# w_out's second parts, the expert choice and expert 0's preparation placed otherwise in an encoder kernel on one core

## The chip, the core and the metric

The kernel runs on one core of a Trainium2 chip. The core has TensorE (PE, matrix products, with a queue of its own for weight loads), VectorE (DVE), ScalarE (ACT), GpSimd (POOL) and SyncE (SP, whose queue issues most of the transfers); each works through its own instructions in order and waits on semaphores for the others. The metric is the time of one execution on the device in microseconds (us), taken as the median of several.

## The reference, cut to what matters

One layer of an encoder runs over two request groups, 512 and 1024 tokens of 1024 channels, with shared weights, all in float32:

```python
h   = rmsnorm(x, norm1_g)
z   = h @ w_in                                # conv value, conv gate, pooling input
yc  = silu(layernorm(depthwise_conv31(za * sigmoid(zg)) + conv_b))
yp  = (centred_mean(zp, windows 2, 4, 8, 16) - zp) @ pool_w * pool_scale
x   = x + concat(yc, yp) @ w_out
h   = rmsnorm(x, norm2_g)
p   = softmax(h @ w_router)                   # 16 experts
gates, idx = top_k(p.T, 2 * tokens // 16)     # each expert picks 64 or 128 tokens of a group
ye  = (silu(h[idx] @ w_gate) * (h[idx] @ w_up)) @ w_down * gates
x   = x.at[idx].add(ye)
x   = x + sigmoid(x @ w_pg + b_pg) * (p_in @ w_ple)
y   = rmsnorm(x, final_g)
```

## The kernel before, in words

A float32 product is made of three passes: each operand is split into a first part (the value rounded to the form that PE multiplies at full rate) and a second part (the value less the first), and first x first, second x first and first x second are added in PSUM. A split takes a copy on ScalarE (first part) and a subtraction on another engine (second part).

The program is emitted in one order, and each engine runs its own instructions in that order.

- **The projection loop** (24 steps). Each step multiplies tokens by a slice of w_in (L103 to L105) and feeds the convolution. A part of the 31 taps runs on PE (L413), on shifted copies of u: `u_shift` loads u from DRAM four times, shifted by one each (L404, on SP's queue). The other taps run on DVE (L427 to L434). Layer norm over channels is made by `ln_steps`, whose inverse square root is a Newton iteration of small operations on GpSimd (L153 to L156, L527, L528). GpSimd also makes the running sums of the pooling heads (L447) and stores (L488, L547). Within steps 18, 20 and 22, `wo_split` (L574) splits eight rows of w_out, 128x1024 each, three, three and two to a step. The rows arrive in buffers of the pool `stg` (name `st`), loaded by `wo_load` (L572) and, for parts of the conv output, by `y_load` (L557). These loads are on SP's queue too, so a load that waits for a buffer holds what stands behind it.
- **Segments 0 to 47**: the product with w_out (`w_mm`, L606 to L608), twelve products a segment, four segments to each of twelve token blocks. Functions are entered in a table `AT` by segment (`at(segment, function, ...)`) and run in the order in which they were entered, behind the segment's products: the residual add (`x1_half`, L613, DVE), transposes of the sum (`x1_T`, L642, PE), the router (`route`, L661; `route_sum`, L669), its softmax (`softmax`, L671 to L680) and the transposition of the probabilities (`probs_T`, L690 or L693, PE).
- **Expert choice.** `topk_steps` finds the top entries of a list by rounds of three DVE instructions (L702 maximum of eight, L703 their places, L704 strike them out): 16 rounds on the list "s" (tokens of the longer group, 512 wide), 8 on the list "p" (256 wide). At the end of every segment `topk` adds a budget to a credit and emits rounds until the credit is used up; a round is booked at 3 x (0.14 + width / 960) us, which is 2.02 and 1.22. When a list is done, its transposition (`merge_T`, L717 on PE and L719 on DVE), its merge (`merge`, L725, L730 to L734) and the gather of expert 0's tokens (`gather`, L746, GpSimd) are entered for later segments, counted from the one in which it ended.
- **Segments 48 to 71**: the product of the second input with w_ple (`ple_mm`, L990 to L992), six products (two half-blocks of three) a segment, with `ple_T` (L976) for the transposes, `ple_out` (L1001, ACT, for half of the last blocks DVE, L999) for the copies out, and the preparation of expert 0: loads of its weights (`load`, L920), their split (`split_hi` on ACT, L937; `split_lo` on DVE, L946), and the transposes of its tokens (`turn0`, L776 and L778, in four parts, copied out at L781 and L782).
- **Experts**: 16 experts with L1187 (gate and up projection) and L1224 to L1240 (down projection); then the last product, with w_pg, and the final norm.

`weights()` opens three pools in the room that earlier pools leave: the raw expert weights (`raw`) and two for the split ones. A tile that is placed where an older tile lay waits for the older one's last reader.

The names in what follows: `wb` and `st`, split and raw w_out rows; `u`, the conv input; `nm`, the softmax's negative scaled maximum; `fs` and `fp`, the lists' results; `prb` and `pr`, probabilities; `xTe`, expert 0's transposed tokens (and, in the ple part, the second input).

## Time and profile before

| | |
|---|---|
| time of an execution, median of 3 | 2300.36 us (2298.39 to 2300.44) |
| the profiled execution's own time | 2296.16 us |
| its span, first to last instruction | 2294.4 us |
| granted TensorE clock, mean of the span | 0.995 |
| PE busy | 2238.4 us (98%) |
| PE weight loads busy | 1906.6 us (83%) |
| DVE busy | 1734.6 us (76%) |
| ACT busy | 1403.3 us (61%) |
| POOL busy | 271.1 us (12%) |

The profile comes from one execution. Busy time is the time in which an engine has an instruction under way. The places of the stages on the time axis: the projection loop runs to about 303 us, segments 0 to 47 from 303.7 to 478.7, segments 48 to 71 from 478.7 to 527.3, the experts from 528.9 to about 2105. A granted clock of 1.00 means TensorE's full 2.4 GHz, 0.50 the half of it.

### The profile page before, as it was taken

The page shows a single profiled execution, that of the slowest core. Times are in us where ns is not written, and L with a number is a line of the kernel's source. Part 1 is how long each engine was busy: PE and PEld are TensorE (multiplying, and loading weights), DVE is VectorE, ACT ScalarE, POOL GpSimd, SP SyncE. Part 2 cuts the span into 40 slices and gives each one's busy share as a digit, 9 for nine tenths or more (in the row PEclk, how much of TensorE's full clock was granted, in tenths as well). Part 3 has the DMA queues.
Part 4 walks back from the last instruction along what each step waited for, and adds up shares of the span by engine and source line. Part 5 has one row for each costly group of instructions (what it writes and reads, how often), then busy time and mean ns, then how long its engine had stood idle before and what let it go on. Part 6 is the DMA issues. An engine that isn't in the chain of part 4 may idle for free.

```text
span 2294.4 us, 36978 instructions
## 1 busy us (share of the span) xinstructions
PE 2238.4 (98%) x15062; PEld 1906.6 (83%) x15106; DVE 1734.6 (76%) x2326; ACT 1403.3 (61%) x1835; POOL 271.1 (12%) x534
## 2 busy tenths in 40 slices
PE   7999999989999999999999999999999999999997
PEld 6888867768798988889898888979888897988675
DVE  8798863667787878778787877878787777878565
ACT  4324336447666766766676676666666767666443
POOL 0122232221001010100101010010101001000321
PEclk9999999999999999999999999999999999999999
DMA  6434555557777677777767777777777777667442
GB/s 199 109 115 123 170 160 188 184 217 265 282 259 277 260 266 280 244 280 265 269 268 260 281 248 274 272 262 267 262 280 255 268 278 256 272 243 275 142 138 101
DMA packets 168874, 534.26 MB, mean 233 GB/s; under 512 B 11969, under 2 KB 38625, under 8 KB 168704
## 3 DMA queue, kind: packets, MB, share of 16 engines
q1 hardware_dynamic: 156064, 493.70, 58.7%
q0 software_dynamic: 9040, 31.46, 5.6%
q10 hardware_dynamic: 3600, 6.74, 0.8%
q8 instruction: 118, 1.93, 0.3%
q14 instruction: 52, 0.43, 0.1%
HBM read 481.34 MB, written 50.52 MB: 232 GB/s over the span
## 4 chain that ended last, share of the span: by engine, by line
PE 77%; issue 10%; DVE 5%; DMA 4%; ACT 2%; POOL 1%; SPq 0%; DVEq 0%; ACTq 0%; POOLq 0%
PE pg L1187 27%; PE pg L1191 13%; PE S L1224 9%; PE Pp L1224 4%; PE S L1234 4%; PE Pp L1240 2%; PE pz L103 2%; PE pz L105 2%; PE pz L104 2%; PE pz L413 2%; PE po L1377 1%; PE po L1376 1%; PE po L1379 1%; DMA u<-u_d 1%; PE pz L606 1%
## 5 line engine op out<-in xcount | busy, mean ns | idle before, releaser
L946 DVE TENSOR_TENSOR wl<-raw,wh 128x2048 bf16<-128x2048 f32 x388 | 881.8, 2283 | 62.8 <-issue 54.9
L1187 PE MATMUL pg<-xTe,wh 128*128 128x384 f32 x4096 | 775.7, 340 | 2.6 <-ACT wp L1001 1.6
L937 ACT ACTIVATE wh<-raw 128x2048 fp32r<-128x2048 f32 x388 | 736.0, 1909 | 39.2 <-DMA raw<-in_w_up_dram 21.9
L1187 PEld LDWEIGHTS pg<-xTe,wh 128*128 128x128 f32 x4096 | 699.9, 188 | 9.4 <-ACT ye_s L1289 6.2
L1191 PE MATMUL pg<-xTb,wl 128*128 128x192 bf16 x4096 | 382.8, 247 | 0.0
L1191 PEld LDWEIGHTS <-wl 128*128 128x128 bf16 x4096 | 325.2, 98 | 40.3 <-issue 40.3
L1250 ACT ACTIVATE t<-pg 128x384 f32<-128x384 f32 x256 | 125.8, 491 | 298.9 <-PE pg L1191 284.1
L1224 PE MATMUL S<-wh,hT 128*128 128x512 f32 x1024 | 285.5, 398 | 0.6 <-ACT ye_s L1289 0.6
L1251 DVE TENSOR_TENSOR t<-pg,t 128x384 f32<-128x384 f32 x256 | 142.7, 557 | 157.7 <-ACT t L1250 157.4
L1224 PEld LDWEIGHTS S<-wh,hT 128*128 128x128 f32 x1024 | 186.4, 188 | 36.8 <-ACT ye_s L1289 1.0
L103 PE MATMUL pz<-xTh,wb 128*128 128x256 f32 x576 | 165.4, 287 | 0.6 <-ACT xTh L212 0.4
L104 PE MATMUL pz<-xTl,wb 128*128 128x256 f32 x576 | 163.0, 283 | 1.5 <-DVE xTl L213 1.5
L105 PE MATMUL pz<-xTh,wb 128*128 128x256 f32 x576 | 163.0, 283 | 0.7 <-DVE wb L241 0.7
L1224 PE MATMUL Pp<-wh,hT 128*128 128x512 f32 x512 | 161.0, 390 | 0.8 <-DVE ye_p L1293 0.8
L746 POOL DMA_INDIRECT xg_s<-h_s,idx_s x16 | 24.2, 1514 | 1160.8 <-PE pg L778 579.1
L429 DVE SCALAR_TENSOR_TENSOR acc<-u,kT,acc 128x496 f32<-128x496 f32 (+2 forms) x168 | 126.9, 755 | 5.1
L103 PEld LDWEIGHTS pz<-xTh,wb 128*128 128x128 f32 x576 | 110.3, 192 | 10.9 <-issue 5.8
L1224 PEld LDWEIGHTS Pp<-wh,hT 128*128 128x128 f32 x512 | 96.1, 188 | 22.4 <-DVE ye_p L1293 1.2
L782 DVE SCALAR_TENSOR_TENSOR xTe<-pg,vT,xTe 128x128 fp32r<-128x128 f32 (+1 forms) x120 | 49.5, 412 | 86.0 <-ACT xTe L781 83.9
L104 PEld LDWEIGHTS pz<-xTl,wb 128*128 128x128 f32 x576 | 110.4, 192 | 1.9 <-DVE xTl L213 1.7
L105 PEld LDWEIGHTS pz<-xTh,wb 128*128 128x128 f32 x576 | 110.4, 192 | 0.9 <-DVE wb L241 0.9
L1234 PE MATMUL S<-wl,hTb 128*128 128x512 bf16 x480 | 108.8, 379 | 2.2
(293 smaller groups left out, 2652.7 us busy)
## 6 DMA issues: line engine op xcount, KB each, us to landing
raw<-in_w_gate_dram SPq DMA_DIRECT2D x128, 1024.0 KB, 6.5
raw<-in_w_up_dram SPq DMA_DIRECT2D x128, 1024.0 KB, 7.9
raw<-in_w_down_dram SPq DMA_DIRECT2D x128, 1024.0 KB, 6.2
u<-u_d SPq DMA_DIRECT2D x32, 262.0 KB, 5.8
st<-yT_d SPq DMA_DIRECT2D x12, 512.0 KB, 5.6
pl<-ple_d SPq DMA_DIRECT2D x12, 512.0 KB, 4.6
out_dram<-raw SPq DMA_DIRECT2D x11, 512.0 KB, 2.9
st<-in_w_out_dram SPq DMA_DIRECT2D x8, 512.0 KB, 4.9
```

The source lines that it names most:

```text
L103: nc.tensor.matmul(out, wh, xh, start=first, stop=False)
L104: nc.tensor.matmul(out, wh, xl, start=False, stop=False)
L105: nc.tensor.matmul(out, wl, xh, start=False, stop=last)
L429: nc.vector.scalar_tensor_tensor(acc[:, :n], u[:, s:s + n], kT[:, c, s:s + 1], acc[:, :n], op0=OP.mult, op1=OP.add)
L937: nc.scalar.activation(h, src, AF.Copy)
L946: nc.vector.tensor_sub(l, src, h.bitcast(F32))
L1187: nc.tensor.matmul(pg[:, f, 0:384].rearrange("p (a t) -> p a t", a=2), h[:, k, f * P:(f + 1) * P], xT[:, k, :, c], start=(k == 0), stop=False)
L1191: nc.tensor.matmul(pg[:, f, 0:192], l[:, k, f * P:(f + 1) * P], xb[:, k, c], start=False, stop=(k == KD - 1))
L1224: nc.tensor.matmul(out[:, n, :], x, rhs(h, i, n), start=(k == 0 and first), stop=(out is Pp and k == KF - 1))
L1234: nc.tensor.matmul(S[:, n, :], hT[1][:, k, so:so + CS], rhs(l, i, n), start=False, stop=(k == KF - 1))
L1250: nc.scalar.activation(t, pg[:, :, 192:384], AF.Copy)
L1251: nc.vector.tensor_add(t, pg[:, :, 0:192], t)
```

## The change

Seven edits in one file:

1. `wo_split`: the subtraction of the eight w_out rows is issued to GpSimd instead of DVE.
2. `softmax`: the product `nm * r` of two 128x1 tiles is written as tensor_scalar, with `r` as the scalar operand, instead of tensor_mul.
3. `topk`: the budget of a segment is 2.9 us instead of 2.35 up to segment 47, and 2.5 instead of 1.25 from 48 on. The 16 rounds of list "s" then end in segment 45 instead of 47, the 8 of list "p" in 55 instead of 58; the entries that are counted from there move with them (`merge_T` "s" from segment 52 to 49, its merge and gather from 54 to 51; `merge_T` "p" from 60 to 56, its merge and gather from 61 to 57).
4. `probs_T` of blocks 8, 9 and 10 is entered one segment later, `h2_out` of block 11 one segment earlier.
5. `turn0`: parts 0 to 3 in segments 66, 67, 68, 69 instead of 68, 69, 68, 70. The loads of the first expert weights: segments 50, 51, 52, 54, 57, 60, 64 instead of 52, 58, 55, 52, 62, 64, 68. `weights()` in segment 48 instead of 50, with the pool `raw` opened first, so that it lies lowest.
6. A new function `sig_table` in segment 56: a sigmoid of one column, whose result nobody reads.
7. The PSUM pools psD and psG of the expert phase are opened in the other order.

```diff
--- before.py
+++ after.py
@@ -577,7 +577,7 @@
         h, l = WO[k // 3][0][:, k % 3, :], WO[k // 3][1][:, k % 3, :]
         r = WOR.pop(k)
         nc.scalar.activation(h, r, AF.Copy)
-        nc.vector.tensor_sub(l, r, h.bitcast(F32))
+        nc.gpsimd.tensor_sub(l, r, h.bitcast(F32))
 
     LATER = (4, 5, 6, 7, 10, 11)
     X, O, HT, LG, PR, RR = {}, {}, {}, {}, {}, {}
@@ -672,7 +672,7 @@
         pl, r = LG.pop(i), RR[i]
         nm = small.tile([P, 1], F32, name="nm")
         nc.vector.tensor_reduce(nm, pl, axis=AX.X, op=OP.max, negate=True)
-        nc.vector.tensor_mul(nm, nm, r)
+        nc.vector.tensor_scalar(nm, nm, r, None, op0=OP.mult)
         pr = prb[:, i % 2, 32:48] if i in LATER else small.tile([P, NE], F32, name="pr")
         sm = small.tile([P, 1], F32, name="sum")
         nc.scalar.activation(pr, pl, AF.Exp, bias=nm, scale=r, accum_out=sm)
@@ -1063,10 +1063,15 @@
     def weights():
         nonlocal hlp, hlp2, rawp
         lft.close()
+        rawp = lpool("raw", 2)
         hlp = lpool("hl", 4)
         hlp2 = lpool("hl2", 6)
-        rawp = lpool("raw", 2)
         WPL["o2"] = lpool("po", 1, lpo).tile([P, 2, D], F32, name="wo2")
+
+    def sig_table():
+
+        t = small.tile([P, 1], F32, name="nm")
+        nc.scalar.activation(t, g1T[:, 0:1], AF.Sigmoid)
 
     OB = 14
     for i in range(12):
@@ -1087,10 +1092,10 @@
         at(max(a + 5, t + 2), route, i)
         at(max(a + 5, t + 2) + 1, route_sum, i)
         at(max(a + 6, t + 3), softmax, i)
-        at(max(a + 7, t + 1), h2_out, i)
+        at(max(a + 7 - i // 11, t + 1), h2_out, i)
         if i < 8:
             at(max(a + 12, t + 1), w_load, i + 4)
-        at(t + 5 if i not in (7, 11) else a + 7 + i // 11, probs_T, i)
+        at(t + 5 if i < 7 else a + 8 if i > 7 else a + 7, probs_T, i)
         if i == 7:
             at(a + 7, list_add, "s")
         elif i == 11:
@@ -1099,10 +1104,11 @@
                     (6, conv1, (2, 3)), (8, conv2, (2, 3)), (8, conv_out, (2, 3)), (6, pool_mm, (2, 3)), (10, open_b, ()),
                     (5, y_load, (2,)), (11, y_prep, (2,)), (14, y_load, (3,)), (20, y_prep, (3,)),
                     (24, y_load, (4,)), (25, y_prep, (4,)), (28, y_load, (5,)), (33, y_prep, (5,)),
-                    (33, ple_load, ()), (41, ple_split, ()), (50, weights, ()),
+                    (33, ple_load, ()), (41, ple_split, ()), (48, weights, ()),
                     (62, split_hi, (0,)), (64, split_lo, (0,)), (64, split_hi, (1,)), (66, split_lo, (1,)),
                     (79, split_hi, (2,)),
-                    (68, turn0, (0,)), (69, turn0, (1,)), (68, turn0, (2,)), (70, turn0, (3,))):
+                    (66, turn0, (0,)), (67, turn0, (1,)), (68, turn0, (2,)), (69, turn0, (3,)),
+                    (56, sig_table, ())):
         at(g, f, *a)
     for q, steps in ((3, (0, -1)), (4, (4, 10, 6, 6, 10, 10)),
                      (5, (15, 13, 14, 14, 16, 16)), (6, (17, 22, 25, 21, 24, 23))):
@@ -1112,7 +1118,7 @@
         at(43 + i if i < 3 else 43 + 2 * i, ple_T, i)
         at(49 + 2 * i, ple_out, i)
     for q in range(8):
-        at((52, 58, 55, 52, 62, 64, 68, 97)[q], load, q // 4, (q % 4,))
+        at((50, 51, 52, 54, 57, 60, 64, 97)[q], load, q // 4, (q % 4,))
 
     z_out(2, 3, 1)
     conv2(2, 2)
@@ -1128,7 +1134,7 @@
             ple_mm(*divmod(seg - 48, 2))
         for f, a in AT.pop(seg, []):
             f(*a)
-        topk(2.35 if seg < 48 else 1.25, seg)
+        topk(2.9 if seg < 48 else 2.5, seg)
         seg += 1
     ps_ab.close()
     ps_stack.close()
@@ -1170,8 +1176,8 @@
         hep = rpool("he", 1, sc)
         ev = rpool("ev", 2, sc)
         ev1 = rpool("ev1", 1, sc)
+        ps_d = sc.enter_context(tc.tile_pool(name="psD", bufs=1, space=PSUM))
         ps_g = sc.enter_context(tc.tile_pool(name="psG", bufs=2, space=PSUM))
-        ps_d = sc.enter_context(tc.tile_pool(name="psD", bufs=1, space=PSUM))
 
         hT = None
         sil = None
```

On GpSimd, end of the projection loop (steps 18 to 22; one piece of the difference, + is of the changed kernel):

```order
 L528 TENSOR_SCALAR ln_nb<-ln_nb 128x2
+L580 TENSOR_TENSOR wb<-st,wb 128x1024 x3
 L488 DMA yT_d<-yc 128x512
 L447 TENSOR_TENSOR ws<-z 128x527
 L447 TENSOR_TENSOR ws<-ws 128x525
 L547 DMA yT_d<-lb 128x4x256
+L580 TENSOR_TENSOR wb<-st,wb 128x1024 x2
 L488 DMA yT_d<-yc 128x512
```

Three subtractions now stand in step 20 between the layer norm's last small operation (L528) and the store and sums behind it, and two in step 22 ahead of its store; three more stand alike in step 18.

On DVE, around the residual add of block 10's second half, while list "s" is worked off (one piece of the difference; L702 to L704 are a round):

```order
 L704 MATCH_REPLACE prS<-fs,prS 48x512
 L613 TENSOR_TENSOR wb<-wb,pz 128x512
+L702 MAX fs<-prS 48x8
+L703 MAX_INDEX is<-fs,prS 48x8
+L704 MATCH_REPLACE prS<-fs,prS 48x512
 L702 MAX fs<-prS 48x8
```

One round more stands behind this add, and so ahead of block 11's first add; with two more rounds further up, two more stand ahead of block 10's first add and three ahead of block 11's.

On PE, behind the last block's probabilities (L690; L990 to L992 are a half-block of the ple product; one piece of the difference):

```order
 L690 MATMUL pt<-ident,prb 48x128
-L717 MATMUL pt<-ident,fs 128x48 x2
-L990 MATMUL pz<-wph,ph 128x512
-L991 MATMUL pz<-wph,pl 128x512
-L992 MATMUL pz<-wpl,ph 128x512
-L990 MATMUL pz<-wph,ph 128x512
```

The transposition of list "s" (L717) no longer follows L690; it stands three segments earlier. Of the eight half-blocks that stood between L690 and the transposition of list "p", four are left.

## Rows read from the trace of the kernel before

**Rows 1.** PE by stretch: stretch, length and busy us, instructions, granted clock, DMA share, GB/s.

```profile
239.00:247.00 8.00, 4.80 (x42) 1.00 0.62 192
462.60:466.00 3.40, 2.79 (x9) 0.50 0.31 125
489.90:496.70 6.80, 5.90 (x16) 0.50 0.89 316
575.00:2000.00 1425.00, 1423.08 (x9677) 1.00 0.73 266
```

**Rows 2.** PE's waits, 200 to 545 us: tile, line, ended by; us, times, longest.

```profile
PE pz L413 <- DMA u<-u_d: 7.9, 4, 3.8
PE pt L693 <- DVE pr L680: 3.0, 1, 3.0
...
PE pt L717 <- ACT xTe L981: 1.7, 1, 1.7
...
PE pt L776 <- DVE xTe L782: 1.5, 1, 1.5
...
PE pg L1187 <- DVE t L1251: 1.1, 1, 1.1
```

**Rows 3.** Timeline of GpSimd: start, us, line, operation, out<-in [idle before <-ended by].

```profile
252.78 1.13 POOL L153 TENSOR_TENSOR nw_t<-nw_y 128x2 f32<-128x2 f32 x1 [11.10 <-DVE nw_y L162]
...
256.26 0.19 POOL L156 TENSOR_TENSOR nw_y<-nw_y,nw_t 128x2 f32<-128x2 f32 x1
...
259.02 0.19 POOL L528 TENSOR_SCALAR ln_nb<-ln_nb 128x2 f32<-128x2 f32 x1
...
457.54 4.55 POOL L970 TENSOR_TENSOR wpl<-wp,wph 128x2048 fp32r<-128x2048 f32 x1 [0.45 <-PE pt L642]
```

**Rows 4.** SyncE's queue at step 20 (timeline), and landing times of all u copies (L404).

```profile
256.68 2.76 SPq L404 DMA_DIRECT2D u<-u_d  x4
...
DMA to landing us min/median/max: 3.4/5.6/10.1
```

**Rows 5.** Timeline of DVE, at step 20 and from 454 to 506 us.

```profile
252.63 3.50 DVE L580 TENSOR_TENSOR wb<-st,wb 128x1024 fp32r<-128x1024 f32 x3
...
454.09 0.68 DVE L702 MAX8 fs<-prS 48x8 f32<-48x512 f32 x1
...
456.37 0.69 DVE L702 MAX8 fs<-prS 48x8 f32<-48x512 f32 x1
...
458.81 3.30 DVE L675 TENSOR_TENSOR nm<-nm,rr 128x1 f32<-128x1 f32 x1
...
470.77 0.69 DVE L613 TENSOR_TENSOR wb<-wb,pz 128x512 f32<-128x512 f32 x1
...
491.45 0.41 DVE L702 MAX8 fp<-prP 48x8 f32<-48x256 f32 x1
...
492.94 0.42 DVE L702 MAX8 fp<-prP 48x8 f32<-48x256 f32 x1
...
505.30 0.22 DVE L708 COPY fp<-fp 48x128 f32<-48x128 f32 x1
```

**Rows 6.** Timeline of PE, at step 20 and from 456 to 529 us.

```profile
268.07 3.64 PE L413 MATMUL pz<-u,diag 128*32 128x512 f32 x32 [0.52 <-issue]
...
456.82 0.63 PE L642 MATMUL pt<-ident,wb 128*128 128x128 f32 x4
...
475.40 0.63 PE L642 MATMUL pt<-ident,wb 128*128 128x128 f32 x4
...
488.80 0.27 PE L690 MATMUL pt<-ident,prb 128*48 128x128 f32 x1 [1.14 <-DVE prb L680]
...
506.07 0.32 PE L717 MATMUL pt<-ident,fp 48*128 48x48 f32 x2
...
528.86 1.46 PE L1187 MATMUL pg<-xTe,wh 128*128 128x384 f32 x7 [1.55 <-ACT wp L1001]
```

**Rows 7.** Timeline of ScalarE, the first sigmoid of the experts.

```profile
539.63 1.28 ACT L1257 ACT_TABLE_LOAD   x1
```

## The prediction

> **What bounds the kernel now.** I read the share of each engine by stretch first [rows 1]: from 575 to 2000 us, the expert phase, TensorE (PE) is busy 1423.08 of 1425 us at the full granted clock. The change touches nothing there, so it can only be worth what PE idles, or runs at half clock, before about 545 us. The waits of PE up to there come next [rows 2]: 7.9 us in four waits for the shifted copies of u, 3.0 for the probabilities of block 9 at L693, 1.7 at L717, 1.5 at L776, and 1.1 at L1187 for a vector operation behind the first sigmoid. PE's own rows add 1.14 us at L690 and 1.55 at the first L1187 [rows 6]. So there are two places: the end of the projection loop (its u copies), and the stretch from 455 to 545 us, where VectorE (DVE) works off the expert choice. The last thing to see is the clock [rows 1]: after the waits of 3 us it was granted at 0.50, that is 1.2 instead of 2.4 GHz, for 3.4 us from 462.6 and for 6.8 us from 489.9, with 2.79 and 5.90 us of PE work in them; from 239 to 247, which begins with 3.2 us of such a wait, it stayed at 1.00. Half of that work, 1.4 and 2.95 us, is lost time; so a new wait of some us costs 0 to 3 us more than itself, and I take 1.5.
>
> **w_out's second parts on GpSimd: +8.0 us.** DVE did three subtractions of 128x1024 in 3.50 us, 1.17 each [rows 5], and there are eight. GpSimd never did one of that size; its 128x2048 form of the same operation took 4.55 us [rows 3], which halves to 2.28, and with 0.1 us between two I take 2.38. DVE gets 9.4 us back, which buys nothing, since no wait of PE in this stretch ends with DVE [rows 2]. What costs is the SyncE queue: the buffer of each w_out row is freed by its subtraction, and the loads into these buffers stand ahead of the four u copies (L404) in that queue.
>
> At step 20 of the loop GpSimd first runs 15 small operations, a Newton iteration and what hangs on it, 252.78 to 259.21 [rows 3]. The first took 1.13 us, and the fourth began only at 256.26, because DVE's subtractions ran then; from there on they begin 0.25 us apart. Without the disturbance the first three take 0.75 instead of 3.48 us, and the chain ends at 256.5. The three subtractions follow, to 256.5 + 3 x 2.38 = 263.6. On DVE the last one ended at 256.13 [rows 5] and L404 began at 256.68 [rows 4], 0.55 later; now it begins at 264.2, 7.5 us later. PE began on these u copies at 268.07, having waited 0.52 us [rows 6], 11.4 us after the first issue. One copy lands in 3.4 to 10.1 us, median 5.6 [rows 4]. At the shortest, the four issues (2.76 us) and a fast landing give 264.2 + 2.8 + 3.4 = 270.4; if it goes as before, 264.2 + 11.4 = 275.6. So PE starts 2.3 to 7.5 us later. I take +5.5, nearer the upper end, since the same loads go into the queues just ahead of the copies as before. PE arrives no later than before, and GpSimd's L488 and L447, now behind the subtractions, delay DVE and ScalarE by 5 us, which lies inside PE's wait. At step 18 two subtractions stand before the copies; GpSimd may begin them before DVE could, or at the same time: 0 to 2 x 1.2 = 2.4 us, I take 0.6. Step 22 is alike, with 0.4. Behind the wait of some 6 us the clock may fall: 1.5. Sum 5.5 + 0.6 + 0.4 + 1.5 = **+8.0** (2.5 to 13).
>
> **L675 by another form.** One product of 128x1, usually 0.16 us, took 3.30 us at 458.81 [rows 5]: it ended when GpSimd's 4.55 us subtraction of 457.54 did [rows 3]. That is the 3.0 us wait at L693 and the 1.4 us of clock. The new form reads one tensor and takes the other as a scalar. No row shows that form inside a GpSimd subtraction, so its price is 0.16 to 3.3 us; I take 0.16, since the operation blocked on GpSimd at 252.78 and this one have in common that DVE reads two tensors from SBUF.
> The Trainium skill, "SBUF — State Buffer", section "Who interferes with whom", says that tensor_scalar can also take the port pair it shares with GpSimd, and that the later of two then blocks fully. By that rule the product would still wait, and the sum would be 3.1 us higher (rival 3); no row here decides it.
>
> **Larger portions (2.35 and 1.25 to 2.9 and 2.5).** A round of the 512-wide list takes 2.28 us and one of the 256-wide list 1.49 [rows 5]. The first list's 16 rounds end two segments earlier. For that, two more rounds stand before block 10's residual add (L613), and three more before block 11's. Block 10's add ended at 454.1, where the next round begins [rows 5]; two rounds at about 2.2 us, as they overlap what follows, make 458.5, while PE wants it at 456.82 [rows 6]: a wait of 1.6. Block 11's began at 470.77 [rows 5], ending 471.5; + 6.6 - 3.1 (L675) is 475.0, while PE, at 475.40 before [rows 6], comes at 475.4 - 3.0 - 1.4 + 1.6 = 472.6: up to 2.4, I take 1.7, since the adds follow the rounds at varying distance. Both together +3.3 (2 to 4). Gone are 3.0 + 1.4, and the 1.14 at L690 (no round stands before block 11's softmax any more). The first list's L717 and L725 now stand ahead of this L690 (+0.4). So the last L690 comes at 488.8 - 5.5 + 3.3 + 0.4, **1.8 earlier**; I take 1.6.
>
> Behind this L690 the second list can begin. Before, eight half-blocks of the ple product (L990 to L992) lay between it and L717 of that list, 488.80 to 506.07 [rows 6]; less the 1.7 us wait and 2.95 of clock that is 12.6, 1.57 each. DVE's last copy ended at 505.52 [rows 5], and PE waited for nothing. Now four half-blocks lie between, 6.3 us; DVE needs about 0.8 to get the transposed probabilities, 8 x 1.49 = 11.9 for the rounds and 0.4 for two copies, 13.1. **A new wait of 6.8 us at L717**, plus 1.5 for the clock.
>
> **Expert 0: the other moves.** From that L690 to the first L1187 took 40.06 us [rows 6]. Without the waits of 1.73 (L717), 1.50 (L776) and 1.55 (L1187), and the 2.95 of clock, 32.3 is left. The transposes of expert 0 go one to a segment, with time for ScalarE and DVE between: the 1.50 goes. Weights are mostly loaded 2 to 7 segments earlier, into buffers that w_out's tiles leave, so that they come no later, and the table load of 1.28 us at 539.63 [rows 7] is done before the experts; PE's 1.1 at L1187 [rows 2], which hangs on the sigmoid behind it, goes. SyncE has the same loads and stores to issue, the loads earlier among the stores. With the PSUM pools in the other order the first L1187 still comes behind the last ple copies: 0.7 of the 1.55 goes, because one of the two readers it waited for is of the other bank now. After: 32.3 - 0.4 + 6.8 + 1.5 + 0.85 = 41.05, +1.0. So the late part is -1.6 + 1.0 - 1.1 = **-1.7** (-4 to +3, the upper end with a blocked L675). The swap costs nothing in the expert phase itself: PE idles 2 us in 1425 there.
>
> **Sum.** +8.0 - 1.7 = +6.3 us. The profiled run took 2296.16 (span 2294.4, 1.8 around it), 4.2 below the median of the runs, 2300.36; so 2302.5 beside it, and **2306.7** as a median. 0.2%, 4.6 us, is about what a measurement of this kernel tells from no change.
>
> **Rivals.** (1) Not slower: SyncE isn't held. Place: the u copies of step 20. If the last subtraction ends by 257, because GpSimd runs them ahead of the Newton chain and at DVE's speed, PE waits no more than before and the 8.0 goes: 2300.4 - 1.7 = 2298.7. Against it stand the order of instructions on GpSimd and the 4.55 us of the larger form. 15%. (2) Not slower: the second list's wait doesn't come. It decides whether DVE is through 13.1 us behind L690, before PE has done its half-blocks; if rounds took half the time on what is already there, or PE were held elsewhere, 6.8 and 1.5 go: 2298.4. Against it: a round of maxima needs all probabilities. 12%. (3) L675 still waits. GpSimd's large subtraction follows a Newton chain that starts behind two more rounds, 4.4 us later, and so runs from about 462 to 466; L675 of block 9 falls at about 463, and 3.1 us come back on DVE before block 11's add: 2309.8. For it, the 3.30 us row; against it, that the new form reads one tensor. 18%. (4) Both (1) and (2), and so faster: 2290. 8%. (5) The forecast, both waits and a free L675: 47%, from 2300 to 2312.
>
> **How the numbers follow.** Faster by over 0.2% (under 2295.8): rival 4 (0.08) and the lower parts of rivals 1 and 2 (0.11): 0.19. Within 0.2% (up to 2305.0): the rest of these (0.16) and the forecast's low end (0.10): 0.26. Slower: 0.55. Range 2294.5 to 2313: out of it fall rival 4, the lowest part of rivals 1 and 2, and the top of rival 3, 0.19.
>
> **What would show it.** L580 on GpSimd near 2.3 us; the four L404 of step 20 issued near 264 and PE's L413 at 272 to 276 with a wait of 5 to 9 us; L675 at 0.16 us throughout; waits of 1 to 2.4 us at L642 of blocks 10 and 11; a wait of about 7 us at L717 near 494 us; no table load behind 530 us; none of the 1.5 us at L776. I'd be wrong by the largest terms if L404 issues before 260, if either new wait is under 3 us, or if the expert phase shows PE idle.

## The result, and the profile after

The changed kernel takes 2315.8 us (2314.41 to 2321.33), the kernel before 2300.4 beside it: a ratio of 1.0072 (1.0053 to 1.0091), 0.7% slower. Slower was forecast, but 2306.7, and 2315.8 lies above the range. The profiled execution took 2314.41 (span 2312.6) against 2296.16, so the two traces have 18.2 us to explain where 6.3 were forecast; the medians are 15.4 apart. Lines behind L1070 stand 6 further down in the changed kernel: its L1193 is the L1187 of before, its L1257 the L1251.

Where the 18.2 us come in is seen by taking the same PE instruction in both timelines:

| PE instruction | before | after | later by | forecast by there |
|---|---|---|---|---|
| first L413 of step 18 | 242.52 | 243.89 | 1.4 | 0.6 |
| first L413 of step 20 | 268.07 | 276.72 | 8.65 | 6.1 |
| first L606, segment 0 | 303.71 | 313.58 | 9.9 | 8.0 |
| first L606, segment 42 | 453.81 | 464.21 | 10.4 | 8.0 |
| first L606, segment 46 | 472.40 | 488.28 | 15.9 | |
| last L690 | 488.80 | 504.03 | 15.2 | 6.4 |
| first L1187 / L1193 | 528.86 | 546.17 | 17.3 | 7.4 |
| end of the span | 2294.4 | 2312.6 | 18.2 | 6.3 |

Of the first 1.4, 0.7 was there long before step 18: the granted clock of the changed kernel's run dipped at 18.5 us, in work that the change doesn't touch. Nor need all of the 9.9 at segment 0 be the change's: nine kernels of the experiments below have the projection loop of the kernel before (a_sub_dve, the four named a1_, b_675_scalar, b_ple_pieces, b_exp0, v1), and in their traces segment 0 begins at 304.8 to 309.4 us, so the 303.71 of this one profile is early. From segment 0 to the end of the span the change costs 8.4 us in this pair, where the forecast had a gain of 1.7.

PE's waits of the changed kernel, 200 to 560 us, answer to [rows 2] (columns as there):

```profile
PE pz L413 <- DMA u<-u_d: 12.9, 3, 7.7
PE pt L717 <- DVE fp L708: 7.2, 1, 7.2
PE pt L976 <- ACT xTe L981: 4.1, 1, 4.1
PE pz L413 <- issue: 2.9, 1, 2.9
...
PE pt L693 <- DVE pr L680: 1.7, 1, 1.7
PE pt L642 <- DVE wb L613: 1.3, 1, 1.3
PE pg L1193 <- ACT wp L1001: 1.1, 1, 1.1
...
PE pt L776 <- DVE xTe L782: 0.2, 1, 0.2
```

The two waits that were forecast are the first two rows. The third row was in no step of the forecast. The fourth stands at step 22, where PE had waited 3.8 us for u before. Then the clock, to [rows 1]: stretches at 0.50 and the expert phase (stretch, length and PE's busy us, instructions, granted clock, DMA share, GB/s).

```profile
243.80:247.20 3.40, 3.31 (x16) 0.50 0.41 130
271.10:281.30 10.20, 4.58 (x24) 0.50 0.55 121
305.20:308.60 3.40, 3.40 (x20) 0.50 0.02 5
479.30:486.10 6.80, 5.00 (x13) 0.50 0.19 77
513.40:523.70 10.30, 6.24 (x18) 0.50 1.03 419
575.00:2000.00 1425.00, 1425.00 (x9705) 1.00 0.73 267
```

Each of the five stretches at half clock begins while PE stands in one of the waits above or just behind it. They hold 22.5 us of PE's work, half of which, 11.3 us, is lost. Before, there were three, the two of [rows 1] and this one, together 12.1 us of work and 6.0 lost:

```profile
295.34:298.74 3.40, 3.40 (x20) 0.50 0.03 7
```

**Step 20 of the projection loop**: SyncE's queue, GpSimd and PE (timelines: start, us, line, operation, out<-in, in brackets the idle time before), to [rows 3], [rows 4] and [rows 6].

```profile
244.88 17.43 SPq L557 DMA_DIRECT2D st<-yT_d  x2
264.30 2.71 SPq L572 DMA_DIRECT2D st<-in_w_out_dram  x2
267.18 2.23 SPq L404 DMA_DIRECT2D u<-u_d  x4
```

```profile
255.78 0.18 POOL L153 TENSOR_TENSOR nw_t<-nw_y 128x2 f32<-128x2 f32 x1 [15.47 <-DVE nw_y L162]
...
259.52 7.11 POOL L580 TENSOR_TENSOR wb<-st,wb 128x1024 fp32r<-128x1024 f32 x3
```

```profile
276.72 5.91 PE L413 MATMUL pz<-u,diag 128*32 128x512 f32 x32 [7.67 <-DMA u<-u_d]
```

In the kernel before the two loads of `st` had stood there for 10.03 us:

```profile
244.22 10.03 SPq L557 DMA_DIRECT2D st<-yT_d  x2
```

Three subtractions take 7.11 us; the two loads now stand 17.43 us in SyncE's queue, because their buffers come free with the subtractions; the four copies of u are issued behind them, and PE waits 7.67 us. The L413 products that follow took 5.91 instead of 3.64 us, at half clock.

**Segments 44 to 48**: DVE, GpSimd, ScalarE and PE, to [rows 5] and [rows 6].

```profile
473.24 0.21 DVE L675 TENSOR_SCALAR nm<-nm,rr 128x1 f32<-128x1 f32 x1
...
474.18 2.39 DVE L680 TENSOR_SCALAR pr<-pr,sum 128x16 f32<-128x16 f32 x1
...
478.66 0.67 DVE L613 TENSOR_TENSOR wb<-wb,pz 128x512 f32<-128x512 f32 x1
```

```profile
471.97 4.57 POOL L970 TENSOR_TENSOR wpl<-wp,wph 128x2048 fp32r<-128x2048 f32 x1 [0.45 <-issue]
```

```profile
479.36 1.06 ACT L619 ACTIVATE wb<-wb 128x1024 f32<-128x1024 f32 x1 [3.89 <-DVE wb L613]
...
480.68 0.37 ACT L981 ACTIVATE xTe<-pt 128x256 f32<-128x256 f32 x1
```

```profile
476.72 0.27 PE L693 MATMUL pt<-ident,pr 128*16 128x128 f32 x1 [1.66 <-DVE pr L680]
481.11 0.69 PE L976 MATMUL pt<-ident,xTe 128*128 128x128 f32 x2 [4.12 <-ACT xTe L981]
...
504.03 0.27 PE L690 MATMUL pt<-ident,prb 128*48 128x128 f32 x1
...
517.46 0.42 PE L717 MATMUL pt<-ident,fp 48*128 48x48 f32 x2 [7.17 <-DVE fp L708]
```

L675 now takes 0.21 us in the midst of GpSimd's large subtraction; but L680, two instructions behind it, stands until GpSimd is through at 476.54. Then a round of the expert choice comes first, and block 11's residual add L613 begins at 478.66. ScalarE waits 3.89 us for it at L619, and behind L619 in its queue stand the copies L979 and L981 that free the buffer in which PE's L976 wants to write. So a late DVE reaches PE by way of ScalarE.

### The profile page after: what moved, and what is told of

It reads as the page before. It is cut to its first block, busy times and chain, and to the rows that moved or that the text cites. A ratio compares the mean times of both kernels' runs of the same rounds, so it can differ in the third digit from the quotient of the medians.

```text
span 2312.6 us, 37023 instructions
## 1 busy us (share of the span) xinstructions
PE 2246.5 (97%) x15106; PEld 1909.8 (83%) x15106; DVE 1727.0 (75%) x2318; ACT 1403.4 (61%) x1836; POOL 287.6 (12%) x542
## 4 chain that ended last, share of the span: by engine, by line
PE 80%; issue 9%; DVE 4%; DMA 4%; ACT 2%; POOL 1%; SPq 0%; DVEq 0%; ACTq 0%; POOLq 0%
PE pg L1193 27%; PE pg L1197 13%; PE S L1230 9%; PE Pp L1230 4%; PE S L1240 4%; PE pz L103 3%; PE pz L104 2%; PE pz L105 2%; PE Pp L1246 2%; PE pz L413 2%; PE po L1382 2%; PE po L1383 2%; PE po L1385 2%; DMA u<-u_d 1%; PE pz L606 1%
## 5 line engine op out<-in xcount | busy, mean ns | idle before, releaser
L1193 PE MATMUL pg<-xTe,wh 128*128 128x384 f32 x4096 | 775.7, 340 | 1.7 <-ACT wp L1001 1.1
L1193 PEld LDWEIGHTS pg<-xTe,wh 128*128 128x128 f32 x4096 | 699.9, 188 | 8.7 <-ACT ye_s L1295 6.2
L1257 DVE TENSOR_TENSOR t<-pg,t 128x384 f32<-128x384 f32 x256 | 142.7, 557 | 159.1 <-ACT t L1256 159.0
L1240 PE MATMUL S<-wl,hTb 128*128 128x512 bf16 x512 | 116.1, 380 | 0.0
```

The lines of the kernel that those rows point to most:

```text
L1193: nc.tensor.matmul(pg[:, f, 0:384].rearrange("p (a t) -> p a t", a=2), h[:, k, f * P:(f + 1) * P], xT[:, k, :, c], start=(k == 0), stop=False)
L1240: nc.tensor.matmul(S[:, n, :], hT[1][:, k, so:so + CS], rhs(l, i, n), start=False, stop=(k == KF - 1))
L1257: nc.vector.tensor_add(t, pg[:, :, 0:192], t)
```

## Experiments

Each ratio is to the kernel before, timed beside it on the same chip, with its 95% interval; differences in us are the ratio's part above or below 1, times 2298, about the median of the kernel before there. A difference of 1 to 4 us between two of these kernels is at best just clear of the noise that their intervals show; there the waits in the traces carry the reading. The theory was: two separate places (SyncE's queue in the projection loop; the larger portions in the late part), plus a lock between DVE and GpSimd (a DVE instruction stands until a running GpSimd one ends) that moves rather than goes.

### The two places apart

**a_sub_dve**: the changed kernel with the subtraction back on DVE.

```diff
-        nc.gpsimd.tensor_sub(l, r, h.bitcast(F32))
+        nc.vector.tensor_sub(l, r, h.bitcast(F32))
```

> The changed kernel with w_out's second parts back on DVE, all else as changed. Theory (two separate places): the first segment begins where it began before, 9.9 us earlier than in the changed kernel (303.7 instead of 313.6), the waits and half-clock stretches behind it stay as in the changed kernel, so about 2306 (2304 to 2308). Rival (what is gained early is lost again, since DVE comes less ahead of PE later): the first segment begins 9.9 us earlier, but the waits between 450 and 525 us grow, 2309 or more.

1.0041 (1.0027 to 1.0055), +9.4 us. The late waits stayed as they were: 7.3 at L717, 4.1 at L976, 1.7 at L693, 1.3 at L642. Segment 0 began at 308.41 us and not at the 303.7 that was expected.

**b_sub_gps**: the kernel before with only the subtraction on GpSimd.

```diff
-        nc.vector.tensor_sub(l, r, h.bitcast(F32))
+        nc.gpsimd.tensor_sub(l, r, h.bitcast(F32))
```

> The kernel before with w_out's second parts on GpSimd and nothing else. Theory (SyncE is held by the buffers that GpSimd frees late): the u copies of step 20 are issued near 267 us, PE waits 7 to 8 us for them and the clock is halved for up to 10 us behind it; the first segment begins 9 to 10 us later and the whole takes 2310 (2308 to 2312). Rival (the late part of the kernel before has slack for a late PE, because there it waits for DVE): under 2306.

1.0040 (1.0026 to 1.0054), +9.2 us. The expected 2310 was missed, since the kernel before took 2297.24 beside it and not 2300.4; the difference is the one expected. Its SyncE timeline at step 20, and its longest waits up to 310 us:

```profile
245.45 17.70 SPq L557 DMA_DIRECT2D st<-yT_d  x2
265.13 2.71 SPq L572 DMA_DIRECT2D st<-in_w_out_dram  x2
268.00 2.24 SPq L404 DMA_DIRECT2D u<-u_d  x4
```

```profile
PE pz L413 <- DMA u<-u_d: 12.1, 3, 8.6
```

The early cost stands alone and is the same as in the changed kernel. Together the two are 18.6, the whole change measured 16.5 (12.2 to 20.9): they add up within the interval, so the places are separate, and each is about half. So the late part, which was forecast to give back 1.7 us, costs 9.4.

### Is it GpSimd's speed, or SyncE's order?

**b_u_first**: the kernel before, with the loads of `st` issued behind the product that needs the u copies, so that they stand behind L404 in SyncE's queue. Subtractions on DVE.

```diff
-        if it in YL:
-            y_load(YL.index(it))
...
-        if 16 <= it <= 16 + 4 and (it - 16) % 2 == 0:
-            for k in range(3 * (it - 16) // 2, min(KD, 3 * (it - 16) // 2 + 3)):
-                wo_load(k)
...
+        if it in YL:
+            y_load(YL.index(it))
+        if 16 <= it <= 16 + 4 and (it - 16) % 2 == 0:
+            for k in range(3 * (it - 16) // 2, min(KD, 3 * (it - 16) // 2 + 3)):
+                wo_load(k)
```

> The kernel before with the same loads behind the u copies, subtractions on DVE. Theory (the order on SyncE's queue costs the kernel before something too: of its 7.9 us of waits for u, those of steps 20 and 22 hang on it): 2 to 5 us less, 2293 to 2296. Rival (these waits are the copies' own landing time of 6 to 10 us): no change.

0.9963 (0.9951 to 0.9976), -8.5 us, more than the 2 to 5 expected. No wait for u is left up to 310 us, and no stretch at half clock between 21.4 and 458.3 us.

**b_gps_u_first**: the same order and the subtraction on GpSimd.

```diff
-        nc.vector.tensor_sub(l, r, h.bitcast(F32))
+        nc.gpsimd.tensor_sub(l, r, h.bitcast(F32))
...
```

> The kernel before with w_out's second parts on GpSimd, and the loads of w_out's rows and of the first conv outputs issued behind the u copies of the same step instead of ahead of them. Theory (SyncE's queue, held by buffers that GpSimd frees late, is what makes the u copies late): PE's wait for the u copies of step 20 falls from 8.6 to under 2 us, the half clock behind it goes, and the 9 us that the subtractions cost alone are down to 0 to 3: 2297 to 2300. Rival (what costs is that GpSimd's sums L447 now stand behind the subtractions, for which DVE and ScalarE stood 8 us): 2304 or more.

0.9958 (0.9943 to 0.9972), -9.7 us. GpSimd's subtractions of step 20 and SyncE there:

```profile
254.39 7.12 POOL L580 TENSOR_TENSOR wb<-st,wb 128x1024 fp32r<-128x1024 f32 x3
```

```profile
249.21 1.75 SPq L404 DMA_DIRECT2D u<-u_d  x4
251.06 6.15 SPq L557 DMA_DIRECT2D st<-yT_d  x2
```

The subtractions take as long as in the changed kernel (7.12 and 7.11 us), and the loads still stand 6.15 us for their buffers. But now no copy of u stands behind them: of the waits for u 0.4 us is left, and 2.0 at L413 for ScalarE (z, L383). The rival is out as well, for GpSimd's sums L447 stand behind the subtractions here too (262.06). So the slower engine costs time only through the order in SyncE's queue: the same edit costs 9.2 us with the one order, and with the other its kernel can't be told from the one with the subtraction on DVE (0.9958 and 0.9963). The expectation had only hoped for the loss to go. That it became a gain fits the 7.9 us that the kernel before already waited for u [rows 2].

**after_u_first**: the same reordering in the whole changed kernel.

```diff
-        if it in YL:
-            y_load(YL.index(it))
...
+        if it in YL:
+            y_load(YL.index(it))
...
```

> The changed kernel, whole, with the loads of w_out's rows and of the first conv outputs issued behind the u copies of the same step. Theory (the early loss of the change hangs on the order of SyncE's queue alone, and the late loss has nothing to do with it): the whole early loss of 9 us goes and the 9 us that this order gives the kernel before come as well, so 17 to 19 us less than the changed kernel, 0 to 2 us under the kernel before; PE's waits between 450 and 525 us stay as they are (1.3, 1.7, 4.1, 7.2). Rival (with PE earlier, the late waits grow): 3 to 8 us above the kernel before.

1.0002 (0.9993 to 1.0012), +0.5 us: 16 us less than the changed kernel, from one move in the source, with the late waits in place (7.2, 4.1, 1.6, 1.3). Against b_u_first (-8.5), which has the same order, that is 9.0 us more: the late part a second time.

### L675 and the lock

**b_675_scalar**: the kernel before with only the other form of the product.

```diff
-        nc.vector.tensor_mul(nm, nm, r)
+        nc.vector.tensor_scalar(nm, nm, r, None, op0=OP.mult)
```

> The kernel before with L675 written as tensor_scalar, nothing else. Theory (GpSimd's 4.55 us subtraction doesn't block the 128x1 form, but does block the tensor_scalar of 128x16 at L680, 1.1 us behind it): L675 takes 0.2 us, L680 of block 9 about 2.2 us until the subtraction ends, PE's wait of 3.0 at L693 shrinks only to 2 to 2.5: the same within 2 us, 2295 to 2298. Rival (tensor_scalar isn't blocked at all): the wait at L693 and the half clock behind it go, 4 us less, about 2293.

0.9994 (0.9985 to 1.0004): no difference. The two lines over the whole run (engine, operation, times; ns min/median/max, first and last start):

```profile
L675 DVE TENSOR_SCALAR nm<-nm,rr x12: 213/214/215, 370.0 to 489.1; 128x1 f32<-128x1 f32 x12
```

```profile
L680 DVE TENSOR_SCALAR pr<-pr,sum x6: 233/234/2400, 370.9 to 462.3; 128x16 f32<-128x16 f32 x6
```

All twelve L675 are free; one L680 takes 2.40 us, and PE's wait at L693 is 2.1 instead of 3.0.

**b_ple_pieces**: the kernel before with GpSimd's large subtraction L970 cut in four.

```diff
-        nc.gpsimd.tensor_sub(WPL["l"], WPL["r"], WPL["h"].bitcast(F32))
+        for q in range(4):
+            c = slice(q * 256, (q + 1) * 256)
+            nc.gpsimd.tensor_sub(WPL["l"][:, :, c], WPL["r"][:, :, c], WPL["h"].bitcast(F32)[:, :, c])
```

> The kernel before with GpSimd's subtraction of 128x2048 (L970) cut into four of 128x512 in columns, nothing else. Theory (the blocked instruction waits until the running GpSimd instruction ends, not longer): L675 of block 9 waits 1.2 us at most instead of 3.1, PE's wait at L693 falls from 3.0 to about 1, the half clock behind it goes: 2 to 4 us less, 2293 to 2295. Rival (the four follow so closely that DVE gets no turn between them): no change, 2297.

1.0002 (0.9981 to 1.0024): in time inconclusive. In the trace the four pieces took 5.01 us instead of 4.55, 1.26 to 1.30 each, L675 1.29 instead of 3.30, L680 0.51, and PE waited 1.3 at L693 instead of 3.0. So the lock lasts as long as one GpSimd instruction; what that is worth in time was not resolved.

### The late part

**a1_first_back**: a_sub_dve, with the first portion back at 2.35.

```diff
-        topk(2.9 if seg < 48 else 2.5, seg)
+        topk(2.35 if seg < 48 else 2.5, seg)
```

> w_out's second parts on DVE, and the portion of a segment up to 47 back at 2.35 us; the portion from 48 on stays at 2.5. Theory (the larger first portion makes DVE late for block 10's and 11's adds): the waits of 1.3 at L642 and 4.1 at L976 go, with the half clock behind them, so 5 to 8 us less than with the portion of 2.9: 2298 to 2301; the wait of 7 us at L717 stays. Rival (GpSimd's large subtraction blocks L680 for 2.2 us and this alone makes the waits): 2 us less at most, 2304 or more.

1.0031 (1.0021 to 1.0041): 2.3 us less than a_sub_dve, about what the rival said. The waits at L642 and L693 went, against the rival, but 3.5 at L976 and 8.0 at L717 stayed. The 5 to 8 us of the theory were too many: it had put the 4.1 at L976 down to the portion alone.

**a1_second_back**: a_sub_dve, with the second portion back at 1.25.

```diff
-        topk(2.9 if seg < 48 else 2.5, seg)
+        topk(2.9 if seg < 48 else 1.25, seg)
```

> w_out's second parts on DVE, and the portion of a segment from 48 on back at 1.25 us; the first stays at 2.9. Theory (the larger second portion only brings the list's transposition ahead of its rounds): the wait of 7.2 us at L717 goes, and with it the half clock of 10.2 us behind it (5.1 us), so 10 to 12 us less than with 2.5: 2294 to 2297. Rival (the wait only moves, to the transposes of expert 0 in segments 66 to 69, which need the second list's tokens): 2300 or more, with a wait of several us at L776 or L778.

1.0036 (1.0023 to 1.0048): only 1.1 us less, which can't be told from nothing, where 10 to 12 were expected. The 7.3 at L717 went. In its place came PE's waits of 2.9 and 2.0 (200 to 560 us), the first for ScalarE, which waits for a store:

```profile
PE pz L990 <- ACT wp L1001: 2.9, 1, 2.9
PE pt L778 <- DMA xg_p<-h_p,idx_pp: 2.0, 1, 2.0
```

```profile
510.74 1.09 ACT L1001 ACTIVATE wp<-pz 128x512 f32<-128x512 f32 x2 [8.61 <-DMA ple_d<-wp]
```

In the changed kernel the same wait of ScalarE is there (its timeline, with the moved table load behind it):

```profile
514.52 1.08 ACT L1001 ACTIVATE wp<-pz 128x512 f32<-128x512 f32 x2 [7.60 <-DMA ple_d<-wp]
...
516.17 1.28 ACT L1074 ACT_TABLE_LOAD   x1
```

It ends before PE's wait at L717 does, at 517.46, and costs nothing. The rival's time came (2300 or more): something else is next late, though the longest new wait is at L990 and not at L776 or L778.

**a1_loads_back**: the former, with the loads of the first expert weights where they were before.

```diff
-        at((50, 51, 52, 54, 57, 60, 64, 97)[q], load, q // 4, (q % 4,))
+        at((52, 58, 55, 52, 62, 64, 68, 97)[q], load, q // 4, (q % 4,))
...
```

> w_out's second parts on DVE, the second portion back at 1.25 us and the loads of expert 0's weights back in their old segments; the first portion stays at 2.9. Theory (four loads of 1 MB within 4 us hold back the stores of the ple product and with them ScalarE, which had stood 8.6 us at L1001 for one): that wait and PE's 2.9 us at L990 go, 3 to 5 us less than with the loads early (2306.1): 2301 to 2303. Rival (the stores wait for something else, and the loads cost nothing): 2305 to 2307.

1.0023 (1.0013 to 1.0033): 3 us less than a1_second_back. PE's 2.9 at L990 is gone (2.1 and 1.2 at L776 and 0.9 at L717 are there instead), and ScalarE's wait for the store is 2.04 instead of 8.61:

```profile
509.32 0.60 ACT L1001 ACTIVATE wp<-pz 128x512 f32<-128x512 f32 x1 [2.04 <-DMA ple_d<-wp]
```

So what held the store were the weight loads issued among the stores. In the changed kernel four of them leave SyncE within 3.4 us (its timeline), and behind 513 us the DMA engines are moving 419 GB/s (last but one row of the clock's view above):

```profile
505.82 0.38 SPq L920 DMA_DIRECT2D raw<-in_w_gate_dram  x1
506.25 0.46 SPq L1002 DMA_DIRECT2D ple_d<-wp  x1
506.76 1.27 SPq L920 DMA_DIRECT2D raw<-in_w_gate_dram  x2
508.07 0.60 SPq L1002 DMA_DIRECT2D ple_d<-wp  x1
508.72 0.52 SPq L920 DMA_DIRECT2D raw<-in_w_gate_dram  x1
```

**a1_small**: both portions and the loads as before, the rest of the change kept, subtractions on DVE.

```diff
-        at((50, 51, 52, 54, 57, 60, 64, 97)[q], load, q // 4, (q % 4,))
+        at((52, 58, 55, 52, 62, 64, 68, 97)[q], load, q // 4, (q % 4,))
...
-        topk(2.9 if seg < 48 else 2.5, seg)
+        topk(2.35 if seg < 48 else 1.25, seg)
```

> The changed kernel with subtractions on DVE and both portions and the loads of before: what is left is L675's form, the later transposition of probabilities, expert 0's transposes, the sigmoid, the PSUM pools. Theory (the first portion makes 1.3 of the waits and most of 1.7, the blocked L680 the rest): waits of 3 to 4 us at L976 stay, those at L642 and L693 go, 2 to 4 us less than with the first portion at 2.9 (2303.4): 2299 to 2301. Rival (the larger first portion costs all of it): 2295 to 2297.

1.0008 (0.9999 to 1.0018), +1.8 us, not clear of none. 3.5 us of wait at L976 stay here too, so that wait comes without the larger portions. What makes it isn't told apart here: the later `probs_T` and the earlier `h2_out` are in this kernel, but L680 is also held for 2.43 us.

**b_exp0**: the kernel before with `sig_table`, `turn0` in four segments and the PSUM pools exchanged.

```diff
...
-                    (68, turn0, (0,)), (69, turn0, (1,)), (68, turn0, (2,)), (70, turn0, (3,))):
+                    (67, turn0, (0,)), (68, turn0, (1,)), (69, turn0, (2,)), (70, turn0, (3,)),
+                    (56, sig_table, ())):
...
-        ps_g = sc.enter_context(tc.tile_pool(name="psG", bufs=2, space=PSUM))
...
+        ps_g = sc.enter_context(tc.tile_pool(name="psG", bufs=2, space=PSUM))
```

> The kernel before with the last edits alone: expert 0's transposes one to a segment (67 to 70), the sigmoid in segment 56, psD ahead of psG; loads, portions and all else as before. Theory (these edits are what the change gains): PE's waits of 1.50 at L776, 1.06 at the second L1187 and part of 1.55 at the first go, 3 us less: 2293 to 2295. Rival (DMA-bound there: PE waits for the second list's gathered tokens or the weights instead): within 1 us of before.

1.0005 (0.9995 to 1.0015): nothing, the rival's case, though the 1.1 at L1187 behind the sigmoid is gone. 1.0 at L778 (for the gather), 1.2 at L776 and 2.0 at the first L1193 stand instead. And at the other end of the kernel there is a new wait of PE, which the changed kernel has as well (waits of the changed kernel, 2100 to 2200 us):

```profile
PE po L1382 <- DVE ye_p L1299: 1.6, 1, 1.6
```

It stands in the traces of all nine kernels with exchanged pools (the changed kernel, those made from it, b_exp0 and v3) and in none of the ten without. The nine also have `turn0` moved, which no run separates from the exchange.

### A version that beats both

**v1**: the kernel before with L675's new form, L970 three segments earlier (so that it does not lie over a softmax), and `sig_table`.

```diff
-        nc.vector.tensor_mul(nm, nm, r)
+        nc.vector.tensor_scalar(nm, nm, r, None, op0=OP.mult)
...
-                    (33, ple_load, ()), (41, ple_split, ()), (50, weights, ()),
+                    (33, ple_load, ()), (38, ple_split, ()), (50, weights, ()),
...
-                    (68, turn0, (0,)), (69, turn0, (1,)), (68, turn0, (2,)), (70, turn0, (3,))):
+                    (68, turn0, (0,)), (69, turn0, (1,)), (68, turn0, (2,)), (70, turn0, (3,)), (56, sig_table, ())):
```

> The kernel before with L675 as tensor_scalar, GpSimd's large subtraction (ple_split) entered in segment 38 instead of 41, and the sigmoid in segment 56. Theory (the port that GpSimd's subtraction takes is what DVE and PE lose there): no DVE instruction falls into the subtraction that shares the port, the waits at L693 and the second L1187 go with a half clock, 4 to 6 us less: 2292 to 2294. Rival (the subtraction meets other DVE instructions in segment 38, or PE then waits at L690 and L717 so much longer): 2296 or more.

0.9967 (0.9953 to 0.9981), -7.6 us: the waits at L693 and at the second L1187 are gone.

**v2**: v1, the order of b_u_first and the subtraction on GpSimd.

```diff
-        nc.vector.tensor_sub(l, r, h.bitcast(F32))
+        nc.gpsimd.tensor_sub(l, r, h.bitcast(F32))
...
```

> All that paid, in one kernel: w_out's second parts on GpSimd with the loads behind the u copies (9.8 us less than before by itself), L675 as tensor_scalar with the large subtraction in segment 38 and the sigmoid in segment 56 (7.1 less by themselves). Theory (two separate places, they add): 15 to 17 us less than before, ratio 0.993. Rival (they share a gain, the half clock above all): 10 to 12 us less.

0.9940 (0.9924 to 0.9957), 2285.24 us: 13.8 us faster than the kernel before (12.6 by the two medians), less than the sum of its parts (9.7 and 7.6), and between what the theory and the rival said.

**v3**: v2 with the first portion at 2.9, the moves of `probs_T`, `h2_out`, `turn0` and `weights`, and the PSUM pools exchanged.

```diff
-        topk(2.35 if seg < 48 else 1.25, seg)
+        topk(2.9 if seg < 48 else 1.25, seg)
...
-        at(t + 5 if i not in (7, 11) else a + 7 + i // 11, probs_T, i)
+        at(t + 5 if i < 7 else a + 8 if i > 7 else a + 7, probs_T, i)
...
```

> As the kernel that joins what paid, but with the first portion at 2.9 us, the transposition of probabilities later, expert 0's transposes in 66 to 69, and the PSUM pools in the other order, as the changed kernel has them. What is still open is whether these are to blame, or only the blocked L680. Theory (the lag of DVE behind PE is the portion's own): waits of 1 to 3 us at L642 or L976 between 450 and 475 us stay, with half clock, and the kernel is 3 to 6 us slower than the one that joins what paid. Rival (only the blocked L680 made the lag hurt): within 1.5 us of it, or faster.

0.9969 (0.9957 to 0.9980), 2291.8: 6.6 us slower than v2 beside it, with no lock in the way and SyncE in order. Its waits: 3.8 at L976, 2.9 at L776, 1.3 at L642, 1.6 at L1382.

**v2_probs** and **v2_portion**: v2 with one of these alone.

```diff
-        at(t + 5 if i not in (7, 11) else a + 7 + i // 11, probs_T, i)
+        at(t + 5 if i < 7 else a + 8 if i > 7 else a + 7, probs_T, i)
```

> The kernel that joins what paid, with only the probabilities of blocks 8 to 10 transposed one segment later. Theory (the wait of 3.8 us at L976 is DVE's lag by the larger portion, showing at the next transpose in PE's order): no wait over 1 us at L976, the same time as without the move within 1.5 us. Rival (the move makes it: two ple transposes then stand with one between them, and the third needs the first one's PSUM buffer): 2 to 4 us at L976 and 3 to 5 us slower.

0.9949 (0.9932 to 0.9966), 2285.5: as v2, with 1.3 us at L976.

```diff
-        topk(2.35 if seg < 48 else 1.25, seg)
+        topk(2.9 if seg < 48 else 1.25, seg)
```

> The kernel that joins what paid, with only the first portion at 2.9 us. Theory (the portion makes the lag): 1.3 us at L642 and 2 to 4 us at L693 or L976, half clock behind it, 4 to 6 us slower. Rival (the move of the probabilities makes it): 1.3 us at L642 alone, 0 to 2 us slower.

0.9959 (0.9945 to 0.9974), 2287.25: 3.5 us at L693, none at L642 or L976, and 1.7 us slower than v2_probs beside it, not the 4 to 6 expected. Each move alone leaves one kind of wait; v3, which has both and the other moves, 1.3 at L642 and 3.8 at L976. So a late DVE shows at L693 while `probs_T` stands where it stood (2.1 in b_675_scalar, 3.5 in v2_portion), and at L976 above all once it is moved (3.5 in a1_small, 3.8 in v3).

## Why the prediction was right in direction and too small

The step that failed is the late part, "-1.6 + 1.0 - 1.1 = -1.7": from segment 0 on the change was to give back 1.7 us, and it costs 9.4 by a_sub_dve, which has it alone. Its largest error is one path: block 11's late add was followed to PE's L642 alone ("up to 2.4, I take 1.7"), and it reached PE through ScalarE, as 4.1 us of wait at L976 with 2.5 of half clock behind it. The early part, forecast at +8.0, cost 9.2 by b_sub_gps. So the sign came out right because of the early part; in the late part it was wrong.

Taken by its own steps, 12 of the 18.2 us of the profile are missing in the forecast's 6.3: 1.9 up to segment 0, 7.0 from there to the last L690, 1.1 to the first L1193 and 2.0 behind it.

- **Subtractions on GpSimd: right.** 2.40 us each against 2.38, SyncE held, PE waiting 7.7 (5 to 9 was named). The early part came to 9.1 (9.9 less the 0.7 that was there before), forecast 8.0 (2.5 to 13). One step in it failed: "the chain ends at 256.5". I let the Newton chain of step 20 begin at 252.78, as before, and only shortened it (by 0.1 us too much: it is 14 operations, 0.28 apart, and not 15 and 0.25). It began at 255.78, since PE, after its 3.84 us wait at step 18, ran 3.31 us at half clock, and DVE's input to the chain came later. So L404 was issued at 267.18 instead of 264.2. From there PE began 9.5 us later, between my ends of 6.2 and 11.4.
- **The clock: mis-sized.** I set 1.5 us for each of two new waits, and took 4.35 off for the two stretches of [rows 1] that I thought gone. Measured: 11.3 us lost after, 6.0 before, so +5.2 where about -1.4 was forecast, 6.6 of the missing 12. The 1.5 was the middle of what waits of 3 us had cost, 0 to 3; but around the waits of 7.7 and 7.2 the clock stayed at 0.50 for 10.2 and 10.3 us, with 4.58 and 6.24 us of work in them, and the waits that were to go were replaced by others, so that no stretch went. Of the 6.6, 4.1 lie behind segment 0, where 5.6 were lost after and 4.4 before: 1.3 more, where 2.85 less was forecast. The rest, ahead of it, hangs in part on one profile: the kernel before lost 1.7 us there, the nine kernels with the same loop 1.9 to 5.1, the changed kernel 5.7.
- **L675: right in its own term, wrong for the path.** All twelve take 0.21 us. The reason I gave (it reads one tensor) is not enough, for L680 reads one tensor too and was held for 2.2 us more than its 0.23. Rival 3 is half right: the lock stayed, one softmax line further on. The Trainium skill, "SBUF — State Buffer", section "Who interferes with whom", whose rule I had set against the forecast, sends the reader on for tensor_scalar to conditions in "VectorE: DVE Perf Modes", section "Mode 2×_2P — use both read ports for one tensor": there the operand's outermost dimension of more than one element is halved between the two ports, and must be even, or odd and equal on both sides. Read with that, 16 columns can take the shared port and one has nothing to halve, which fits the two rows (2.39 and 0.21 us); no run tried another width.
- **The larger portions: right in mechanism, too few places.** 1.3 at L642 came (1.6 was forecast for block 10, 1.7 for block 11), and 1.7 instead of 3.0 at L693. The step that failed is "up to 2.4, I take 1.7": I followed block 11's add to PE's own L642 only. The add is waited for by ScalarE as well (L619), and ScalarE's queue holds the copies that free PE's transpose buffer: 4.1 at L976, and 5.0 us of work at half clock behind it. The last L690 came 5.4 later than segment 0 had, where I had it 1.6 earlier; the wait and half of that work are 6.6 of these 7.0. a1_small and v2_probs show that this wait is not the portion's alone: the later `probs_T`, for which the forecast has no term, makes 1.3 of it by itself (v2_probs). The held L680 isn't needed for it (v3 has 3.8 us there without); what `h2_out` does was not run alone.
- **L717: right.** 7.2 against 6.8. What I left out is that it covers the next thing: undone alone it gave back 1.1 us of 9.4, since the early weight loads held ScalarE's stores, and ScalarE with them, for 8.6 us. "The loads earlier among the stores" stood in the forecast without a price; uncovered, it is about 3 us.
- **Expert 0: gains nearly as forecast, and a price at the far end.** L776 went from 1.5 to 0.2, the table load is done at 516.17 in PE's wait, the wait behind the sigmoid fell from 1.1 to 0.5, the one at the first L1193 from 1.55 to 1.15 (0.85 forecast). But "the swap costs nothing in the expert phase itself" stopped at 2000 us, and the last product pays 1.6 for it at L1382.

Of the rivals, (1) and (2) did not come, and so not (4). The forecast's own case came nearest, for both its waits came and L675 is free; but the wait at L976 was in none of the cases. The attribution by runs: the early part about 9, the second portion and the loads together 4 (the portion alone 1.1; the loads were not undone alone), the first portion 2.3 to 3.5, the remaining moves about 2.

What stays open: between the last L690 and the first L1193 the waits and the clock add up to 3.3 us more than before (+5.44 at L717, -1.33 at L776, -0.55 at L991, -0.40 at the first L1193, +0.17 of clock), while 2.1 were measured, and only 0.4 of the difference is work that now lies ahead of L690; and how v2's parts come to 13.8 and not 17.3.

## What to carry to other kernels

Before a step is moved to a slower engine, look at what its buffers free: a load that waits for a buffer holds all that stands behind it in its issuing queue, and with the urgent copies ahead of it both choices of engine came out ahead (-8.5 and -9.7 us), where with the old order the slower one had cost 9.2. When a wait is taken away, name the next instruction with the same need (L680 behind L675, the store behind L717) and the other engine that waits for the same result (ScalarE's L619), since these were what came next. When one profile stands for before, other kernels with the same stage show how typical it is: here the projection loop ended 1 to 6 us later in nine of them. And a wait of several us on PE has to be priced with the half clock behind it, which here cost up to 3 us more.

## What the runs showed of the hardware that was not expected

- The granted clock after like waits differs from run to run: behind the wait of 3.2 us at 239.32 it stayed at 1.00 in the kernel before, but fell to 0.50 between 241 and 246 in seven of the nine kernels whose projection loop is the same (2.8 to 3.5 us of wait there). A single profile of before does not show what such a wait costs.
- A tensor_scalar of 128x1 runs in 0.21 us inside a GpSimd subtraction of 4.57 us, one of 128x16 is held until that ends (2.39 to 2.40 us instead of 0.23).
- GpSimd's subtraction of 128x1024 takes 2.40 us, DVE's 1.22; four pieces of 128x512 take 5.01 where one of 128x2048 takes 4.55.
- With four weight loads issued within 3.4 to 3.6 us among the stores, ScalarE waited 7.6 to 8.6 us for a store, against 2.0 with the loads spread out.
